# A diffusion layer's attention kernel: scratch transfers by pairs of heads

## The chip, the cores and the metric

The kernel runs on one core of one Trainium2 chip. The metric is device time in microseconds of one execution. The kernel before took 641.58 us (median of three runs, 641.37 to 641.83).

## What is computed

One layer over 1024 latent tokens (a grid of 16 rows by 64 columns) and 256 context tokens, model width 1024, in float32. The inputs are normalised and modulated, one projection gives eight groups of 512 columns, and two branches follow: attention in eight heads of 64, and a gated convolution. Cut to what matters here:

```python
h  = rmsnorm(x, norm_g) * (1 + scale) + shift          # (1024, 1024)
q, k, v, za, u, bg, cg, zc = split(h @ w_in)           # eight times (1024, 512)
q, k = rmsnorm(heads(q), q_norm_g), rmsnorm(heads(k), k_norm_g)
kc, vc = split(hc @ w_in[:, 512:1536])                 # context keys and values (256, 512)
# per head: scores of rotated q and k in an 8 x 16 window plus a bias,
# scores of plain q and kc, one softmax over both
s = concat([rope(q) @ rope(k_window) / 8 + bias, q @ kc / 8])
o = softmax(s) @ concat([v_window, vc])
attn = o * silu(za)
conv = bg * conv3(cg * u) * silu(zc)
out  = x + gate * (concat([attn, conv]) @ w_out)
```

## The kernel before

Matrix products keep float32 accuracy by splitting each operand into a high half and the rest (`halves`), and adding two or three products of those halves. A tensor in SBUF therefore often has a dimension of 2 for high and low.

There are four stages.

1. *Preparation.* Modulation, normalisation, transposing of the tokens, and the first convolution group.
2. *Projection of q, k and v.* The loop `for n in range(NT + 3)` runs over 4 pairs of heads times 8 tiles of 128 tokens. `proj_tile` gives a tile's products, `head_scale`, `rms_normed` and `rotated` finish q and k, `turn_qk` transposes them for every second tile, and `normed_ctx` and `turn_kc` do the context's keys and values once a pair. SBUF is full, so the results are spilled to scratch tensors in DRAM: `q_d`, `k_d`, `v_d`, `kc_d`, `vc_d`, one of each for a head. `spill` only notes a store; `flush`, at the next step of the loop, issues it on SP's queue.
3. *Attention.* The loop `for n in range(4 * NH + 4)` runs over quarters of heads, four to a head. `quarter(n)` writes out by hand, for all engines, the order of the work: the scores of quarter n, the exponentials of quarter n-2, the products with v of quarter n-3, and between them steps of `fill`, which are the products of the gate and convolution groups (tile `pu`, weights `uraw`). With `strict` on, TensorE, ScalarE, VectorE and GpSimd keep the written order. A class `head` loads its data from scratch: `load_v` at the head's first quarter, and for the following head `masks` and `load_q` (which also loads kc) in quarter 1 and `load_k` in quarter 2, as written. SP is not held to that order and issues a load when its turn has come and its buffer is free. Buffers for q, k, kc, v and the bias table are double: a head's buffers are those of the head two before it. q, k and kc are loaded twice over, once into partitions 0 to 63 and once into 64 to 127 (for q, the high half below and the low half above), so each of these is a transfer of 64 partitions. v's tile `vts` has 65 columns a block, the last of which holds a 1 in the high part and a 0 in the low part, so that the sum of the exponentials falls out as a 65th row of the product. That column is set once, and the loads fill the other 64 columns in rows of 256 bytes.
   `finish` copies a finished bank and stores it from ScalarE's queue (L1042, L1043). `gated` takes a pair's sums, inverts them, stores them to `ri_d`, and reads them back spread over 64 partitions a head by `load_sums`; the last pair does that on GpSimd's queue, in the fourth stage.
4. *Output projection.* `put_y` and `out_mm`, over two halves of the columns and eight tiles of tokens.

Line 55 is the helper through which ordered instructions are recorded, so many groups carry L55. The lines of the loads are L948 (k), L957 (q), L958 (kc), L965 and L967 (v), L507 (sums) and L295 (uraw).

Of the kernel before, what the change touches and what calls it, by code (L numbers as in the profile page):

```python
# [10 lines left out]
F32 = mybir.dt.float32  # L11
# [8 lines left out]
P = 128  # L20
D = 1024
T = 1024
# [17 lines left out]
def body(tc, es, x, ctxt, w_ada, b_ada, w_in, q_g, k_g, rpbr, w_out, vecs, cst, out):  # L40
# [49 lines left out]
    def many(name, n, shape):  # L90
        return [dr.tile(shape, F32, name=f"{name}{i}")[:] for i in range(n)]
# [9 lines left out]
    zs_d = many("zs_d", NPAIR, [P, T])  # L101


    q_d = many("q_d", NH, [2, HD, 4, 2, 256])
    k_d = many("k_d", NH, [HD, 4, 2, 256])
    v_d = many("v_d", NH, [P, 4, 2, 2 * HD])
    kc_d = many("kc_d", NH, [HD, 2, L])
    vc_d = many("vc_d", NH, [P, 2, 2 * HD])
    ri_d = many("ri_d", NPAIR, [2, T])


# [76 lines left out]
    def halves(dst, lo, src):  # L188
        act.copy(dst, src)
        dve.tensor_tensor(lo, src, dst.bitcast(F32), ALU.subtract)  # L190

    def put_v(vs, i, ps):

        halves(vs[:, :, 0, i], vs[:, :, 1, i], ps.rearrange("p (s d) -> p s d", s=2))

    def normed(qn, ps, scale, n):
        for h in range(n):
# [28 lines left out]
    def turn_qk(pp, p, two, t0):  # L226

        pA = psm.tile([P, 2, 2, P], F32, name="trA", tag="C", bufs=2)
        pB = psm.tile([P, 512], F32, name="trB", tag="C", bufs=2)
        for i, (qn, rot) in enumerate(two):  # L230
            pe.transpose(pA[:, 0, i], rot[:, 0:P], ident)
            pe.transpose(pA[:, 1, i], qn[:, 0:P], ident)
            pe.transpose(pB[:, i * P:(i + 1) * P], rot[:, P:256], ident)

        def put():
            qs = pp.tile([P, 2, 2, 256], F32R, name="qs", tag="qs", bufs=2)
            halves(qs[:, 0], qs[:, 1], pA[:].rearrange("p k i d -> p k (i d)"))
            ks = pp.tile([P, 2, 256], F32R, name="ks", tag="ks", bufs=2)
            halves(ks[:, 0], ks[:, 1], pB[:, :256])
            for s in range(2):  # L240
                h, rows = 2 * p + s, slice(64 * s, 64 * s + 64)
                for l in range(2):
                    spill(q_d[h][l, :, t0 // 2], qs[rows, l])
                spill(k_d[h][:, t0 // 2], ks[rows])
        return put

    def ctx_products(ch):
# [8 lines left out]
        return acc  # L256

    def normed_ctx(pp, acc, scales):
        two = []
        vs = pp.tile([P, 2, 2, 2, HD], F32R, name="vs", tag="vs", bufs=4)  # L260
        for i in range(2):
            qn = pp.tile([P, P], F32, name="kn", tag="kn", bufs=2)
            normed(qn, acc[i], scales[i], 2)
            pool.tensor_tensor(by_head(qn[:]), by_head(qn[:]), gkc.broadcast_to([P, 2, HD]), ALU.mult)
            put_v(vs, i, acc[i][:, P:256])
            two.append(qn)
        return two, vs

    def turn_kc(pp, p, two, vs):
        pB = psm.tile([P, 512], F32, name="trC", tag="C", bufs=2)  # L270
        for i in range(2):
            pe.transpose(pB[:, i * P:(i + 1) * P], two[i], ident)

        def put():
            ks = pp.tile([P, 2, 256], F32R, name="ks", tag="ks", bufs=2)
            halves(ks[:, 0], ks[:, 1], pB[:, :256])
            for s in range(2):
                h, rows = 2 * p + s, slice(64 * s, 64 * s + 64)
                spill(kc_d[h], ks[rows])
                spill(vc_d[h], vs[:, s].rearrange("p l i d -> p l (i d)"))  # L280
        return put

    def proj_tile(ch, t):
# [219 lines left out]
        pool.dma_start(ri_d[p].rearrange("h (x c) -> (h x) c", c=16), ri)  # L503

    def load_sums(f, half, rb, queue):
        for i in range(2):
            queue.dma_start(rb[64 * i:64 * i + 64],  # L507
                            ri_d[f][i:i + 1, half * 512:(half + 1) * 512].broadcast_to([64, 512]))


    prs = ExitStack()
# [421 lines left out]
                stores.append(lambda nh=nh, gr=gr: sp.dma_start(g_d[:, nh * 512:(nh + 1) * 512], gr[0:1]))  # L933


    class head:
        def __init__(self, h):
            self.h, self.p, self.s = h, h // 2, h % 2
# [5 lines left out]
        def load_k(self):  # L944
            h = self.h
            self.k = self.place().tile([P, 4, 2, 256], F32R, name="k_s", tag="A")
            for i in range(2):
                sp.dma_start(self.k[64 * i:64 * i + 64].bitcast(F32), k_d[h])  # L948

        def load_q(self):  # L950
            h = self.h
            self.q = self.place().tile([P, 2, T], F32R, name="q_s", tag="B")
            self.kc = bmp.tile([P, 2, L], F32R, name="kc_s", tag="kc_s", bufs=2)
            for i in range(2):
                rows = slice(64 * i, 64 * i + 64)
                for k in range(2):
                    sp.dma_start(self.q[rows, k].bitcast(F32).rearrange("p (t c) -> p t c", c=256), q_d[h][i, :, :, k])  # L957
                sp.dma_start(self.kc[rows].bitcast(F32), kc_d[h])  # L958

        def load_v(self):  # L960
            h = self.h
            self.v = vts[h % 2]
            for l in range(2):
                for t in range(4):
                    sp.dma_start(self.v[:, l, 2 * t:2 * t + 2, 0:HD].bitcast(F32),  # L965
                                 v_d[h][:, t, l].rearrange("p (b d) -> p b d", d=HD))
                sp.dma_start(self.v[:, l, NB:, 0:HD].bitcast(F32), vc_d[h][:, l].rearrange("p (b d) -> p b d", d=HD))  # L967

        def masks(self):
            self.bt = bmp.tile([P, 3, 384], F32, name="bt", tag="bt", bufs=2)  # L970
# [185 lines left out]
    pps = ExitStack()  # L1156
    pp = pps.enter_context(sbuf("ppn"))
    sq = pp.tile([P, 4, HD + 1], F32, name="sq")
    pool.memset(sq[:, :, HD:], EPS)
    rope = pp.tile([P, 2, NB, 2, HD], F32, name="rope")  # L1160
    sp.dma_start(rope[:].rearrange("p a b k d -> p (a b k d)"), rope_d)
# [8 lines left out]
    for n in range(NT + 3):  # L1170


        p, t = divmod(n, NB)
        at = 2 if p < NPAIR - 1 else 0
        if 1 <= t and p + 1 < NPAIR:
            raws += [chunk_load(CQ + (p + 1) * P, k) for k in ([t - 1] if t < NB - 1 else [t - 1, t])]
        if n == 0:
            loaded[z_col(4)] = unit_load(z_col(4))
        if n == NT - 8:
            loaded[z_col(0)] = unit_load(z_col(0))  # L1180
        if 1 <= n <= KT:
            gate.load(n - 1)
            next(spread, None)
        if 9 <= n < 25 and n % 2:
            next(tables)
        if n == NT - 6:
            heads[0].masks()
            heads[0].load_k()
        if n == NT - 5:
            heads[0].load_q()  # L1190
        flush()

        if t == 0 and 0 < n < NT:
            nxt += map(chunk_split, raws)
            ch, nxt, raws = nxt, [], []
        if n == 0:
            next(group0)
        if n == NT - 4:
            next(fill)
        if n < NT:  # L1200
            tiles[n] = proj_tile(ch, t)
        else:
            for _ in range((4, 3, 1)[n - NT]):
                next(fill)
        if 5 <= n < 9:
            for _ in range(2):
                next(group0)
        if n == 9:
            for _ in group0:
                pass  # L1210
        if 0 < n <= NT:
            scales[n - 1] = head_scale(pp, tiles[n - 1], 4)
            if n % 2:
                vs = pp.tile([P, 2, 2, 2, HD], F32R, name="vs", tag="vs", bufs=4)
            put_v(vs, (n - 1) % 2, tiles[n - 1][:, 256:384])
            if n % 2 == 0:
                q, r = divmod(n - 1, NB)
                for s in range(2):
                    spill(v_d[2 * q + s][:, r // 2], vs[:, s].rearrange("p l i d -> p l (i d)"))
        if t == at + 1 and n < NT:  # L1220
            cscales = [head_scale(pp, a, 2) for a in cacc]

        if 1 < n <= NT + 1:
            m, r = n - 2, (n - 2) % NB
            qn = rms_normed(pp, tiles[m], scales.pop(m))
        while waiting:
            waiting.pop(0)()
        if 4 <= t and p + 1 < NPAIR:
            nxt.append(chunk_split(raws.pop(0)))
        if 1 < n <= NT + 1:  # L1230
            tiles[m] = rotated(pp, rope, qn, r)
        if t == at + 2 and n < NT:
            kc = normed_ctx(pp, cacc, cscales)
        do_dves()
        if 2 <= n < KT + 2:
            gate.add(n - 2)
        if 9 <= n < 25 and n % 2 == 0:
            next(tables)
        do_acts()

        if n == KT + 5:
            gate.sum()
        if t == at and n < NT:
            cacc = ctx_products(ch)
        if n % 2 == 0 and n >= 4:
            waiting.append(turn_qk(pp, (n - 4) // NB, [tiles.pop(n - 4), tiles.pop(n - 3)], (n - 4) % NB))
        if t == at + 3 and n < NT:
            waiting.append(turn_kc(pp, p, *kc))
# [9 lines left out]
    prp = vs_.enter_context(sbuf("prp"))  # L1258
    vts = [prp.tile([P, 2, NB + 2, HD + 1], F32R, name=f"v{i}") for i in range(2)]
    fill_up(prp, 64)  # L1260
    for v in vts:
        for l in range(2):
            pool.memset(v[:, l, :, HD:HD + 1].bitcast(F32), 1.0 - l)

    gating = []

# [176 lines left out]
```

## Time and profile before

| | |
|---|---|
| median of three runs | 641.58 us (641.37 to 641.83) |
| the profiled execution's own time | 643.59 us |
| its span, first to last instruction | 641.8 us |
| instructions | 10295 |
| DMA packets | 118864, 125.46 MB, mean 195 GB/s |
| of these under 512 bytes, under 2 KB | 32817, 89353 |
| granted TensorE clock | 0.999 |

A profile shows one execution. Busy time counts the union of an engine's instructions; a wait is put down to what ended it; the chain is followed backwards from the last instruction through whatever released each step. A row of a view by stretches of time gives the length, the busy time of each engine, the granted clock, the mean busy share of the 16 DMA engines and GB/s.

### The profile page before, as it was taken

What the parts mean: (1) busy time and instruction counts of PE and PEld (TensorE: products, weight loads), DVE (VectorE), ACT (ScalarE), POOL (GpSimd) and SP (SyncE); (2) the same over time, 40 slices, a digit from 0 to 9 for tenths busy, and PEclk for the clock granted to TensorE, in tenths of its full rate; (3) what the DMA queues carried; (4) which work ended last, traced back from release to release, by engine and by line L of the source; (5) the groups of instructions that cost most, each with busy time, mean ns of one, the idle gap of its engine ahead of it and who ended that gap; (6) DMA issues with size and microseconds to landing.
All of it is one profiled execution on the core that took longest, in us unless ns stands there. A gap on an engine that the chain in (4) does not pass through costs nothing.

```text
span 641.8 us, 10295 instructions
## 1 busy us (share of the span) xinstructions
PE 629.1 (98%) x3480; PEld 537.3 (84%) x3480; DVE 432.3 (67%) x819; ACT 322.5 (50%) x692; POOL 131.5 (20%) x138
## 2 busy tenths in 40 slices
PE   8999999999999999999999999999999999999997
PEld 3477899999899999777688878888888888888885
DVE  1677859665756756458697889988998864565111
ACT  3676835424525444346676648565675644352000
POOL 1205024123123222001111211121111111004421
PEclk9999999999999999999999999999999999999999
DMA  8973647867785897899767758885862223965621
GB/s 319 379 257 97 180 121 259 256 188 206 241 260 165 271 269 218 216 221 223 184 160 195 186 140 212 202 214 149 225 150 88 71 81 128 293 235 198 215 100 49
DMA packets 118864, 125.46 MB, mean 195 GB/s; under 512 B 32817, under 2 KB 89353, under 8 KB 117532
## 3 DMA queue, kind: packets, MB, share of 16 engines
q1 hardware_dynamic: 112348, 113.23, 61.4%
q10 hardware_dynamic: 6208, 11.05, 5.5%
q0 software_dynamic: 256, 0.54, 0.3%
q8 instruction: 27, 0.44, 0.3%
q14 instruction: 25, 0.20, 0.1%
HBM read 88.01 MB, written 38.53 MB: 197 GB/s over the span
## 4 chain that ended last, share of the span: by engine, by line
PE 75%; DMA 10%; DVE 8%; SPq 3%; ACT 2%; issue 1%; ACTq 0%; DVEq 0%
PE pacc L55 21%; PE pu L55 18%; PE acc L55 5%; PE pout L76 5%; PE pout L74 5%; PE pout L75 5%; PE po L55 4%; PE tr L55 4%; PE cacc L55 4%; DMA v<-v_d 4%; DMA k_s<-k_d 3%; DVE mx L55 2%; DVE sb L55 2%; PE pss L55 2%; PE pmx L55 2%; DMA slab<-in_w_ada 2%
## 5 line engine op out<-in xcount | busy, mean ns | idle before, releaser
L55 PE MATMUL pu<-h,uh 128*128 128x512 f32 x544 | 169.0, 392 | 0.0
L55 PE MATMUL pacc<-wh,h 128*128 128x384 f32 x512 | 135.1, 338 | 0.0
L55 PEld LDWEIGHTS pu<-h,uh 128*128 128x128 f32 x544 | 98.2, 188 | 17.0
L55 PE MATMUL pu<-h,ul 128*128 128x512 f32 x272 | 106.3, 391 | 0.0
L55 PEld LDWEIGHTS pacc<-wh,h 128*128 128x128 f32 x512 | 92.8, 188 | 0.1
L55 POOL TENSOR_TENSOR plc<-sc,phc 128x512 fp32r<-128x512 f32 x32 | 42.5, 1327 | 222.8 <-ACT sc L55 111.4
L55 PE MATMUL pacc<-wl,h 128*128 128x384 f32 x256 | 85.6, 335 | 0.0
L55 POOL TENSOR_TENSOR ss<-ss,few 128x4 f32<-128x4 f32 (+1 forms) x40 | 42.0, 1051 | 125.8 <-DVE ss L55 125.4
L55 PEld LDWEIGHTS pu<-h,ul 128*128 128x128 f32 x272 | 51.1, 188 | 11.3
L55 DVE TENSOR_TENSOR mx<-mx,sb 128x384 f32<-128x384 f32 (+1 forms) x64 | 55.5, 876 | 1.9
L75 PE MATMUL pout<-wol,yh 128*128 128x512 f32 x128 | 49.8, 389 | 0.0
L76 PE MATMUL pout<-woh,yl 128*128 128x512 f32 x128 | 49.6, 389 | 0.0
L74 PE MATMUL pout<-woh,yh 128*128 128x512 f32 x128 | 48.3, 389 | 0.0
L55 PEld LDWEIGHTS pacc<-wl,h 128*128 128x128 f32 x256 | 48.1, 188 | 0.1
L55 DVE TENSOR_REDUCE ss<-sq 128x4 f32<-128x260 f32 (+1 forms) x40 | 15.7, 393 | 41.9 <-ACT sq L55 41.9
L55 ACT COPY mg<-pmx 128x256 f32<-128x256 f32 x32 | 12.0, 374 | 61.7 <-PE pmx L55 44.5
L55 ACT ACTIVATE sq<-pacc 128x256 f32<-128x256 f32 x32 | 12.3, 385 | 57.1 <-PE pacc L55 56.6
L1375 DVE TENSOR_TENSOR ot<-pout,gate 128x512 f32<-128x512 f32 x16 | 10.8, 688 | 37.6 <-PE pout L76 35.5
L55 DVE TENSOR_TENSOR pll<-sb,phl 128x768 fp32r<-128x768 f32 (+2 forms) x33 | 29.3, 889 | 7.9 <-ACT sb L55 7.9
L55 DVE TENSOR_TENSOR sc<-sc,mg 128x512 f32<-128x512 f32 x32 | 21.8, 683 | 19.0 <-ACT mg L55 19.0
L1376 POOL TENSOR_TENSOR ot<-ot,xr 128x512 f32<-128x512 f32 x15 | 20.0, 1347 | 67.6 <-DVE ot L1375 66.5
L55 ACT ACTIVATE qn<-pacc,ss 128x64 f32<-128x64 f32 x128 | 30.1, 329 | 4.7 <-issue 2.5
(151 smaller groups left out, 1277.0 us busy)
## 6 DMA issues: line engine op xcount, KB each, us to landing
uraw<-in_w_in SPq DMA_DIRECT2D x34, 256.0 KB
q_d<-qs SPq DMA_DIRECT2D x64, 128.0 KB
k_s<-k_d SPq DMA_DIRECT2D x16, 512.0 KB
q_s<-q_d SPq DMA_DIRECT2D x32, 256.0 KB
wr<-in_w_in SPq DMA_DIRECT2D x40, 192.0 KB
slab<-in_w_ada SPq DMA_DIRECT2D x6, 1024.0 KB
t_d<-btw SPq DMA_DIRECT2D x8, 576.0 KB
bt<-t_d SPq DMA_DIRECT2D x8, 576.0 KB
```

What stands on the lines that cost most here:

```text
L55: i = emit(*a, **kw)
L74: i = pe.matmul(ps, ah, bh, start=first, stop=False)
L75: pe.matmul(ps, ah, bl, start=False, stop=False)
L76: pe.matmul(ps, al, bh, start=False, stop=last)
L1375: dve.tensor_tensor(ot, ps, gate[:, cols], ALU.mult)
L1376: (dve if (nh, t) == (1, NB - 1) else pool).tensor_tensor(ot, ot, xr, ALU.add)
```

## The change

The scratch tensors are kept by pairs of heads, with 128 partitions. The stores of q, k and kc go out as one transfer for two heads. v's scratch holds all ten blocks (eight of latent tokens, two of context) with the columns of ones and zeros among them; the tile that is stored has them, and three such tiles are kept and used in turn. A head then loads v in two transfers, each a whole row of 650 numbers a partition. k and kc are read twice over by one transfer, whose source starts with a step of 0 and a count of 2 (`twice`). q's high and low parts come in one transfer for each of its two kinds (rotated and plain), the outermost dimension of whose source is the part. The sums of a pair's two heads are read by one transfer. A head has 7 loads in place of 19: one each of k, kc and the bias table, two of q and two of v.

```diff
-    q_d = many("q_d", NH, [2, HD, 4, 2, 256])
-    k_d = many("k_d", NH, [HD, 4, 2, 256])
-    v_d = many("v_d", NH, [P, 4, 2, 2 * HD])
-    kc_d = many("kc_d", NH, [HD, 2, L])
-    vc_d = many("vc_d", NH, [P, 2, 2 * HD])
+    q_d = many("q_d", NPAIR, [2, P, 4, 2, 256])
+    k_d = many("k_d", NPAIR, [P, 4, 2, 256])
+    v_d = many("v_d", NPAIR, [P, 2, 2, NB + 2, HD + 1])
+    kc_d = many("kc_d", NPAIR, [P, 2, L])
...
+    vss = []
+    def next_vs():
+        vss.append(vss.pop(0))
+        return vss[-1]
+    def spill_v(p, b, vs):
+        spill(v_d[p][:, :, :, b:b + 2].rearrange("p s l b d -> p (s l) (b d)"), vs.rearrange("p s l i d -> p (s l) (i d)"))
...
-            for s in range(2):
-                h, rows = 2 * p + s, slice(64 * s, 64 * s + 64)
-                for l in range(2):
-                    spill(q_d[h][l, :, t0 // 2], qs[rows, l])
-                spill(k_d[h][:, t0 // 2], ks[rows])
+            for l in range(2):
+                spill(q_d[p][l, :, t0 // 2], qs[:, l])
+            spill(k_d[p][:, t0 // 2], ks)
...
-            for s in range(2):
-                h, rows = 2 * p + s, slice(64 * s, 64 * s + 64)
-                spill(kc_d[h], ks[rows])
-                spill(vc_d[h], vs[:, s].rearrange("p l i d -> p l (i d)"))
+            spill(kc_d[p], ks)
+            spill_v(p, NB, vs)
...
     def load_sums(f, half, rb, queue):
-        for i in range(2):
-            queue.dma_start(rb[64 * i:64 * i + 64],
-                            ri_d[f][i:i + 1, half * 512:(half + 1) * 512].broadcast_to([64, 512]))
+        r = ri_d[f]
+        queue.dma_start(rb, bass.AP(r.tensor, r.offset + half * 512, [[T, 2], [0, HD], [1, 512]]))
...
+    def twice(rows):
+        n = 1
+        for step, size in list(rows.ap)[1:]:
+            n *= size
+        return bass.AP(rows.tensor, rows.offset, [[0, 2], [n, HD], [1, n]])
...
         def load_k(self):
-            for i in range(2):
-                sp.dma_start(self.k[64 * i:64 * i + 64].bitcast(F32), k_d[h])
+            sp.dma_start(self.k[:].bitcast(F32).rearrange("p t l c -> p (t l c)"), twice(k_d[self.p][64 * self.s:64 * self.s + 64]))
...
         def load_q(self):
-            for i in range(2):
-                rows = slice(64 * i, 64 * i + 64)
-                for k in range(2):
-                    sp.dma_start(self.q[rows, k].bitcast(F32).rearrange("p (t c) -> p t c", c=256), q_d[h][i, :, :, k])
-                sp.dma_start(self.kc[rows].bitcast(F32), kc_d[h])
+            for k in range(2):
+                sp.dma_start(self.q[:, k].bitcast(F32).rearrange("p (t c) -> p t c", c=256),
+                             q_d[self.p][:, 64 * self.s:64 * self.s + 64, :, k])
+            sp.dma_start(self.kc[:].bitcast(F32).rearrange("p l c -> p (l c)"), twice(kc_d[self.p][64 * self.s:64 * self.s + 64]))
...
         def load_v(self):
             for l in range(2):
-                for t in range(4):
-                    sp.dma_start(self.v[:, l, 2 * t:2 * t + 2, 0:HD].bitcast(F32),
-                                 v_d[h][:, t, l].rearrange("p (b d) -> p b d", d=HD))
-                sp.dma_start(self.v[:, l, NB:, 0:HD].bitcast(F32), vc_d[h][:, l].rearrange("p (b d) -> p b d", d=HD))
+                sp.dma_start(self.v[:, l].bitcast(F32), v_d[self.p][:, self.s, l])
...
+    vss += [pp.tile([P, 2, 2, 2, HD + 1], F32R, name=f"vs{i}")[:] for i in range(3)]
+    for v in vss:
+        for l in range(2):
+            pool.memset(v[:, :, l, :, HD:HD + 1].bitcast(F32), 1.0 - l)
...
-                vs = pp.tile([P, 2, 2, 2, HD], F32R, name="vs", tag="vs", bufs=4)
+                vs = next_vs()
...
-                for s in range(2):
-                    spill(v_d[2 * q + s][:, r // 2], vs[:, s].rearrange("p l i d -> p l (i d)"))
+                spill_v(q, r - 1, vs)
...
-    for v in vts:
-        for l in range(2):
-            pool.memset(v[:, l, :, HD:HD + 1].bitcast(F32), 1.0 - l)
```

More of the change, by code (lines that the diff above doesn't have):

```diff
@@ L190, in halves @@
         dve.tensor_tensor(lo, src, dst.bitcast(F32), ALU.subtract)
+    vss = []
[4 more added lines that the diff above has]
+        spill(v_d[p][:, :, :, b:b + 2].rearrange("p s l b d -> p (s l) (b d)"), vs.rearrange("p s l i d -> p (s l) (i d)"))
     def put_v(vs, i, ps):
-        halves(vs[:, :, 0, i], vs[:, :, 1, i], ps.rearrange("p (s d) -> p s d", s=2))
+        halves(vs[:, :, 0, i, :HD], vs[:, :, 1, i, :HD], ps.rearrange("p (s d) -> p s d", s=2))
     def normed(qn, ps, scale, n):
@@ L258, in normed_ctx @@
     def normed_ctx(pp, acc, scales):
-        two = []
-        vs = pp.tile([P, 2, 2, 2, HD], F32R, name="vs", tag="vs", bufs=4)
+        two, vs = [], next_vs()
         for i in range(2):
@@ L1213, in body @@
             if n % 2:
-                vs = pp.tile([P, 2, 2, 2, HD], F32R, name="vs", tag="vs", bufs=4)
+                vs = next_vs()
             put_v(vs, (n - 1) % 2, tiles[n - 1][:, 256:384])
```

## The prediction

> **What bounds the kernel now.** I read the page first, for the engines' shares and the chain.
>
> ```profile
> span 641.8 us, 10295 instructions
> PE 629.1 (98%) x3480; PEld 537.3 (84%) x3480; DVE 432.3 (67%) x819; ACT 322.5 (50%) x692; POOL 131.5 (20%) x138
> PE 75%; DMA 10%; DVE 8%; SPq 3%; ACT 2%; issue 1%; ACTq 0%; DVEq 0%
> ```
>
> TensorE is busy for 98% of the span and carries 75% of the chain that ended last; transfers carry only 10%. So making transfers cheaper can win little, and making them dear can lose much. Next, the stages: the attention stage cut at each head's first score product, by the busy time in stretches. The columns are length, then busy time of PE, PEld, DVE, ACT and POOL, the granted clock, the mean busy share of the 16 DMA engines, and GB/s.
>
> ```profile
> 270.23 0.48 PE L55 MATMUL pss<-q_s,k_s 128*128 128x256 f32 x2
> 481.88 0.72 PE L55 MATMUL pss<-q_s,k_s 128*128 128x256 f32 x4
> 223.80:270.20 46.40, 46.40 (x273) 44.20 (x272) 24.51 (x69) 20.20 (x75) 9.59 (x15) 1.00 0.88 235
> 270.20:481.90 211.70, 206.24 (x1177) 173.14 (x1175) 178.11 (x271) 136.64 (x223) 34.46 (x30) 1.00 0.77 190
> 481.90:641.80 159.90, 155.41 (x749) 129.27 (x747) 80.53 (x125) 51.84 (x86) 31.68 (x29) 1.00 0.44 146
> ```
>
> Head 0 starts at 270.2 and head 7 at 481.9, so seven heads take 211.7 us, 30.2 us each, or 7.6 us for each of a head's four quarters. In all of it TensorE stands idle for 211.70 - 206.24 = 5.5 us. That is the most that better loads can give back there. Then the chain in order of time, at the places where transfers stand on it, and the queue that issues them.
>
> ```profile
> 279.80 10.59 DMA k_s<-k_d
> 300.89 0.60 SPq L948
> 301.89 11.40 DMA v<-v_d
> 313.31 0.53 ACTq L1043
> 314.21 0.59 ACT sc L55
> 392.23 0.67 SPq L948 DMA_DIRECT2D k_s<-k_d  x1
> 396.08 0.46 SPq L948 DMA_DIRECT2D k_s<-k_d  x1
> 397.78 0.42 SPq L295 DMA_DIRECT2D uraw<-in_w_in  x1
> ```
>
> Two things are to be seen. ScalarE issues the stores of a finished bank (L1043), and it sat there until a v load that SP had queued behind a k load (L948) had landed; only then did its own arithmetic go on. And the weights of the filler products (uraw) are issued right behind the k load of the next head. Whatever holds that load holds those too, and ScalarE, which works in written order, must split them within the same head.
>
> **The change, part by part.** These are the transfers that it touches, with their counts and sizes.
>
> ```profile
> q_d<-qs SPq DMA_DIRECT2D x64, 128.0 KB
> k_s<-k_d SPq DMA_DIRECT2D x16, 512.0 KB
> q_s<-q_d SPq DMA_DIRECT2D x32, 256.0 KB
> v_d<-vs SPq DMA_DIRECT2D x32, 128.0 KB
> v<-v_d SPq DMA_DIRECT2D x64, 64.0 KB
> kc_s<-kc_d SPq DMA_DIRECT2D x16, 128.0 KB
> rb<-ri_d SPq DMA_DIRECT2D x12, 128.0 KB
> rb<-ri_d POOLq DMA_DIRECT2D x4, 128.0 KB, 3.7
> ```
>
> *Edits that I cost at nothing.* The stores of q, k and kc keep their bytes in half as many issues, the same rows. Each v store becomes 520-byte rows, four a partition, in place of 1 KB rows. All of it lies in the projection, where TensorE idles for none of the 46.40 us above; without that cover it would be some tenths of a microsecond a store. The three rotating v buffers in place of four, and six small memsets moved from the start of attention to the start of the projection, stand beside the same products; POOL is 20% busy. The v loads turn from ten of 256-byte rows into two of 2,600-byte rows, and gain at most a part of the 5.5 us. Each now needs its whole buffer free, which is so a quarter before the head starts, four quarters before its first use.
>
> *The loads of q, k, kc and 1/sum.* Here is the choice on which the forecast hangs. Before, each was cut into parts of 64 partitions, and 64 was the outermost count on both sides. Now one instruction fills 128 partitions, but its source pattern begins with a count of two: two copies for k and kc (`[[0, 2], [n, HD], [1, n]]`), the high and low plane for q, the two heads of 1/sum (`[[T, 2], ...]`). No transfer of before has that form at this size, so I bound it. One end: the 16 engines share it as they do now. Other end: the work is dealt out by the outermost count, and two engines carry everything. The nearest rows are four stretches in which the eight loads of the bias rows (248 rows each, whose largest divisor up to 16 is 8) run almost alone, and one in which transfers of 128 rows run.
>
> ```profile
> t_d<-in_rpb SPq DMA_DIRECT2D x8, 23.2 KB
> 72.00:73.00 1.00, 1.00 (x8) 0.84 (x7) 1.00 (x4) 0.49 (x2) 0.00 (x0) 1.00 0.25 28
> 73.00:74.00 1.00, 1.00 (x8) 0.63 (x7) 0.86 (x2) 1.00 (x2) 0.00 (x0) 1.00 0.38 47
> 74.00:75.00 1.00, 1.00 (x7) 0.82 (x6) 0.63 (x1) 1.00 (x3) 0.00 (x0) 1.00 0.30 37
> 75.00:76.00 1.00, 1.00 (x8) 0.87 (x7) 0.74 (x3) 1.00 (x3) 0.00 (x0) 1.00 0.27 33
> 10.00:14.00 4.00, 4.00 (x20) 1.39 (x17) 0.43 (x2) 2.27 (x4) 0.57 (x1) 1.00 1.02 412
> 276.00:292.00 16.00, 15.38 (x82) 12.76 (x81) 10.59 (x18) 10.52 (x17) 1.30 (x1) 1.00 1.00 215
> ```
>
> With 248 rows the share never passes 0.38; eight of 16 engines could give 0.5 at most. With 128 rows it is 1.02. That fits a deal by the outermost count; thin issue would explain it too. I take two engines: the only rows with an outermost count that 16 doesn't divide side with that reading. The Trainium skill says the same outright ("DMA: Bandwidth & Descriptors", section "Rules for kernel authors"): a leading zero-stride broadcast of c copies confines the whole transfer to at most c engines. The stretches above agree, and no run here shows it for two; by that rule the sum is the one below.
>
> *The price.* At full share an engine moves 412 / 16 = 25.7 GB/s (10:14, wide transfers) or 215 / 16 = 13.4 GB/s (276:292, where 64-partition loads crowd). Two engines alone crowd nobody, so I take 25.7. Per head, q is 4 x 256 KB and k 2 x 512 KB, 2,048 KB or 1,024 KB an engine, 1.05 MB: 41 us. kc adds 2 x 128 KB, 5 us: 46 us together, against 30.2 us for a whole head. 1/sum adds 4 x 128 KB a pair, or 5 us a head. These engines also owe their sixteenth of everything else: 190 GB/s over 30.2 us is 5.7 MB, less 2.4 MB of q, k and kc, leaves 3.3 MB, 0.21 MB an engine, 8 us.
>
> *Where it meets the path.* A head's q and k buffers come free when its successor's first scores are done, and only then are they refilled for the head after. So from one head's first scores to the next's lie at least the 46 us and, as an estimate, 3 us of issue, landing and score. The other three quarters do not all fit beside it. ScalarE stands at its bank store in quarter 1 until an older load lands, as at L1043 above, and the uraw behind k lands only after k, so the fillers and everything behind ScalarE stand too. I take two of the four quarters, 15 us, as work left when the loads are in. Period: 46 + 3 + 15 = 64 us, and the 8 us of other traffic runs in those 15. SP's queue stands behind the same landings; 12 fewer issues a head save nothing there.
>
> *Start and end.* Head 0's k load is issued at 223.8:
>
> ```profile
> 223.75 1.48 SPq L55 DMA_DIRECT2D k_s<-k_d  x2
> ```
>
> Its 46 us would just end at 270. But that stretch moves 235 GB/s x 46.4 us = 10.9 MB, of which 8.5 MB are others', 0.53 MB an engine, 20 us. So head 0 starts at 290. After head 7's first scores nothing large is left to load: 159.9 us stay. The last pair's 1/sum, on POOL's queue, goes from 3.7 us a load to 256 KB over two engines, 5 us, twice; it is needed by the seventh of eight rounds of the output products, which hide it.
>
> *Sum.* 290 + 7 x 64 + 160 = 898 us of span, 256 more than 641.8. The profiled execution took 643.6 us, 1.8 over its span and 2.0 over the median of 641.6. So I add 256 to the median: **898 us**.
>
> **The rivals.**
>
> *Well dealt (faster).* The 16 engines share the new transfers. Then 128 partitions an instruction replace pairs of 64, the crowded 13.4 GB/s an engine moves towards 25.7, k lands some 5 us earlier, and up to the 5.5 us of idle goes: 636 to 641 us. For it: the chain's 10.59 and 11.40 us pieces. It decides wherever a leading count of two doesn't limit the engines. The Trainium skill has a rule on this side too (same page and section): two transfers to disjoint partition halves had better be one of 128 partitions. The 13.4 against 25.7 GB/s agrees with it. Chance 0.08, of which 0.02 leave no measurable change (within 0.2%, about what a measurement here can tell).
>
> *Two engines, well hidden.* The transfers alone set the period, everything else fits beside them: 48 us, and head 0 is not late. 270 + 336 + 160 = 766 us. Against it stands ScalarE's wait at L1043. Chance 0.17 for times below 830.
>
> *Two engines, nothing hidden.* Other traffic and 1/sum stand in line as well: 46 + 3 + 13 + 15 = 77, with two and a half quarters left 81: 290 + 567 + 160 = 1017 us. Chance 0.15 for times above 950.
>
> *Two engines at the crowded rate.* 13.4 GB/s: 88 + 3 + 15 = 106 us a head, 290 + 742 + 160 = 1192 us. Against: only two engines write. Chance 0.05.
>
> **How the numbers follow.** The likeliest, 830 to 950 around 898, has 0.55. The range 766 to 1017 takes in the two neighbours and leaves out the well dealt case, the crowded rate and a little beside. Faster 0.06, same 0.02, slower 0.92.
>
> **What would show it.** Right: the k and q loads take some 20 us or more each to land; the DMA share of the attention stage falls from 0.77 to below 0.5 while the stage takes twice as long; TensorE's busy share drops to about 70%, its waits ending in k, q, uraw; the projection and the last 160 us look as before. Wrong: a share that stays at 0.7 or more with k landing in under 10 us means that all engines carry it, and the time is then near 638. A stage that grows by less than 100 us means that more lies beside the loads than I allowed.

## The result, and the profile after

The changed kernel took 918.93 us (median of four runs, 918.33 to 920.23) against 641.71 us before on the same chip: a ratio of 1.432, 95% interval 1.4295 to 1.4345. The forecast was 898 us, with a range of 766 to 1017.

The page of the changed kernel answers to the first lines shown of before (span, busy times, the chain by engine, and issues that were changed, with KB each and, where the trace has it, the median time to landing):

```profile
span 916.6 us, 10016 instructions
PE 655.5 (72%) x3479; PEld 558.7 (61%) x3480; DVE 429.1 (47%) x819; ACT 322.8 (35%) x692; POOL 129.4 (14%) x138
PE 49%; DMA 28%; SPq 12%; DVE 8%; ACT 2%; issue 2%; ACTq 0%; DVEq 0%
k_s<-k_d SPq DMA_DIRECT2D x8, 1024.0 KB
q_s<-q_d SPq DMA_DIRECT2D x16, 512.0 KB
rb<-ri_d POOLq DMA_DIRECT2D x2, 256.0 KB, 14.8
```

Fewer instructions, nearly the same bytes, and 275 us more. TensorE fell from 98% to 72%; on the chain, transfers rose from 10% to 28%, and SP's own issuing from 3% to 12%. The same three stages as before, cut at the first score products of head 0 and of head 7 (columns as in the prediction):

```profile
305.11 0.48 PE L55 MATMUL pss<-q_s,k_s 128*128 128x256 f32 x2
752.38 0.72 PE L55 MATMUL pss<-q_s,k_s 128*128 128x256 f32 x4
222.60:305.10 82.50, 51.76 (x278) 48.59 (x277) 24.23 (x69) 20.35 (x75) 9.72 (x11) 0.79 0.34 120
305.10:752.40 447.30, 227.07 (x1177) 191.23 (x1175) 174.98 (x271) 136.84 (x223) 34.04 (x30) 0.75 0.27 91
752.40:916.60 164.20, 157.02 (x749) 129.01 (x747) 80.72 (x125) 51.77 (x86) 31.27 (x27) 1.00 0.43 142
```

Where the time came from: head 0 starts 34.9 us later (305.1 for 270.2), the seven heads take 235.6 us more (447.3 for 211.7), and the end 4.3 us more (164.2 for 159.9). Together that is 274.8 us, the whole difference of the spans. In the seven heads the 16 engines are busy for 27% of the time, down from 77%, while the arithmetic waits for transfers. That pair, a low share and long waits for data, points to a few full engines and many empty ones. The packet records of the trace agree: for 60% of these 447.3 us exactly two packets are under way; before, it was 1% of the stage.

The waits of ScalarE and VectorE in that stretch (total, times, longest) show which data it was:

```profile
ACT uh L55 <- DMA uraw<-in_w_in: 74.0, 3, 34.8
ACT ub L55 <- DMA zs_d<-zs: 30.1, 1, 30.1
ACT mg L55 <- DMA q_s<-q_d: 22.7, 2, 15.7
DVE zs L55 <- DMA zs<-zs_d: 55.1, 2, 43.9
DVE zs L55 <- DMA rb<-ri_d: 38.4, 2, 32.0
DVE tb L55 <- DMA tb<-o_d: 25.8, 1, 25.8
```

Most of it is waited for weights (uraw) and gate rows (zs, tb), which the change doesn't touch. They stand behind the loads that it does touch, as the experiments below bear out. The 22.7 us ahead of mg are ScalarE standing at its bank store (L1046 in this kernel) until q had landed. And the chain from 218 to 306 us, where head 0's data are fetched, has SP itself as its longest pieces:

```profile
233.07 21.62 SPq L55
254.74 10.76 SPq L55
265.54 2.67 SPq L964
276.26 7.71 DMA k_d<-ks
```

SP was not waiting before an issue there, it stood 21.62 us inside the issue of q's second load and 10.76 us inside that of kc. Meanwhile the projection's stores were not issued, its buffers stayed full (ScalarE waited 31.2 us for a store of v), and TensorE ran for only 51.76 of 82.5 us. Head 0's first score product, at 305.11 above, waited for no data; it came when the late projection was through. In the seven heads the issues in SP's timeline add up to 274 of 447.3 us (106 issues); before, to 101 of 211.7 us (195 issues).

### The profile page after: what moved, and what is told of

Its sections match the earlier page's. It is cut to its first block, busy times and chain, and to the rows that moved or that the text cites. A ratio compares the mean times of both kernels' runs of the same rounds, so it can differ in the third digit from the quotient of the medians.

```text
span 916.6 us, 10016 instructions
## 1 busy us (share of the span) xinstructions
PE 655.5 (72%) x3479; PEld 558.7 (61%) x3480; DVE 429.1 (47%) x819; ACT 322.8 (35%) x692; POOL 129.4 (14%) x138
## 4 chain that ended last, share of the span: by engine, by line
PE 49%; DMA 28%; SPq 12%; DVE 8%; ACT 2%; issue 2%; ACTq 0%; DVEq 0%
PE pacc L55 12%; PE pu L55 12%; SPq L55 6%; DMA q_s<-q_d 5%; DMA zs_d<-zs 4%; DMA ri_d<-ri 4%; PE acc L55 4%; DMA zs<-zs_d 3%; PE po L55 3%; DMA tb<-o_d 3%; PE tr L55 3%; PE cacc L55 3%; DVE mx L55 2%; PE pout L76 2%; PE pout L75 2%; PE pout L74 2%
## 5 line engine op out<-in xcount | busy, mean ns | idle before, releaser
L55 PE MATMUL pu<-h,uh 128*128 128x512 f32 x544 | 171.7, 397 | 22.5 <-ACT ub L55 22.5
L55 PE MATMUL pmx<-ci,mx 128*128 128x128 f32 x64 | 17.1, 322 | 178.1 <-DVE mx L55 177.7
L55 PE MATMUL pacc<-wh,h 128*128 128x384 f32 x512 | 137.6, 343 | 0.0
L55 PEld LDWEIGHTS pmx<-ci,mx 128*128 128x128 f32 x64 | 9.6, 151 | 188.2 <-ACT sb L55 122.6
L55 DVE TENSOR_TENSOR ul<-uraw,uh 128x512 fp32r<-128x512 f32 x34 | 22.7, 683 | 97.2 <-ACT uh L55 97.0
L55 ACT ACTIVATE phc<-sc 128x512 fp32r<-128x512 f32 x32 | 20.2, 633 | 124.4 <-DVE sc L55 124.2
L55 DVE TENSOR_TENSOR mx<-mx,sb 128x384 f32<-128x384 f32 (+1 forms) x64 | 52.2, 824 | 2.0
L55 ACT CAST uh<-uraw 128x512 fp32r<-128x512 f32 x34 | 20.7, 615 | 83.3 <-DMA uraw<-in_w_in 83.2
L55 DVE TENSOR_TENSOR zs<-zs,rb 128x512 f32<-128x512 f32 x6 | 4.1, 689 | 93.5 <-DMA zs<-zs_d 55.1
L55 PE MATMUL pss<-q_s,k_s 128*128 128x384 f32 (+1 forms) x128 | 34.4, 398 | 16.8 <-DMA k_s<-k_d 16.8
```

The costliest lines, as they stand in the source:

```text
L55: i = emit(*a, **kw)
```

## The experiments

Each edit is shown against the changed kernel, unless said otherwise. Times are medians; the ratio is to the kernel before on the same chip, with its 95% interval.

**All loads in halves again.** Pair scratch, 128-partition stores and v's whole rows stay.

```diff
-            sp.dma_start(self.k[:]..., twice(k_d[self.p][64 * self.s:64 * self.s + 64]))
+            for i in range(2):
+                sp.dma_start(self.k[64 * i:64 * i + 64]..., k_d[self.p][64 * self.s:64 * self.s + 64])
...                                                # the same for q (by part), kc and 1/sum
```

> The loads of q, k, kc and 1/sum are cut into two transfers of 64 partitions again, so that no source begins with a count of two; the scratch by pairs, the stores of 128 partitions, v's columns of ones, the three v buffers and the whole-row v loads stay as in the changed kernel. Theory (the leading count of two puts these loads on two of 16 engines): the time falls from 919 us back to 634 to 643 us, the share of the DMA engines in the attention stage is back above 0.6. Rival (something else in the change costs it: the shared scratch of two heads, three v buffers, v loads that need the whole buffer): still above 850 us. A mixture would lie between and tell how much each has.

640.43 us, ratio 0.9973 (0.9959 to 0.9988). Head 0 and head 7 start at 270.4 and 478.7:

```profile
270.40:478.70 208.30, 204.64 (x1176) 173.27 (x1175) 178.12 (x271) 136.68 (x223) 34.81 (x30) 1.00 0.69 188
478.70:638.70 160.00, 155.46 (x750) 129.38 (x748) 80.44 (x125) 51.81 (x86) 31.64 (x29) 1.00 0.45 146
```

The whole loss lies in the form of these loads, and none in the rest. The rest gains 1 to 3 us: the heads take 208.3 us in place of 211.7, with 3.7 us of idle TensorE for 5.5. This version is 0.3% faster than the kernel before.

**The count by itself.** A kernel of loads alone:

```python
dims = [[4096, P], [1, 2048]] if c == P else [[0, c], [4096, P // c], [1, 2048]]
nc.sync.dma_start(big, bass.AP(w_in.tensor, w_in.offset, dims))      # then VectorE reads big
```

> Only loads, one at a time, each waited for by VectorE: the same 1 MB into 128 partitions by rows of 8 KB, from sources whose outermost count is 128, 64, 32, 16, 8, 4 and 2 (all but the first read rows more than once), then the same in two transfers of 64 partitions; all of that twice. The layer isn't computed. Theory (engines are dealt by the outermost count, up to 16): 128 to 16 take the same, 4 to 6 us; 8 takes 7, 4 takes 12, 2 takes 22 us, with DMA shares near 0.5, 0.25 and 0.12 in between; the two halves 5 to 7 us. Rival (all engines share any transfer of 128 partitions): all between 4 and 7 us.

The second round, in the timeline. The wait is the last number; the counts are 128, 64, 32, 16, 8, 4, 2, then the two halves:

```profile
88.74 0.15 DVE L49 COPY few<-big 128x1 f32<-128x1 f32 x1 [4.91 <-DMA big<-in_w_in]
94.09 0.15 DVE L49 COPY few<-big 128x1 f32<-128x1 f32 x1 [5.20 <-DMA big<-in_w_in]
99.51 0.15 DVE L49 COPY few<-big 128x1 f32<-128x1 f32 x1 [5.26 <-DMA big<-in_w_in]
106.99 0.15 DVE L49 COPY few<-big 128x1 f32<-128x1 f32 x1 [7.32 <-DMA big<-in_w_in]
119.18 0.15 DVE L49 COPY few<-big 128x1 f32<-128x1 f32 x1 [12.04 <-DMA big<-in_w_in]
136.61 0.15 DVE L49 COPY few<-big 128x1 f32<-128x1 f32 x1 [17.28 <-DMA big<-in_w_in]
159.12 0.15 DVE L49 COPY few<-big 128x1 f32<-128x1 f32 x1 [22.36 <-DMA big<-in_w_in]
166.79 0.15 DVE L49 COPY few<-big 128x1 f32<-128x1 f32 x1 [7.52 <-DMA big<-in_w_in]
```

In stretches of the first round (counts 128, 8, 4 and 2; here the columns are DVE, POOL, clock, DMA share, GB/s):

```profile
1.50:5.50 4.00, 0.00 (x0) 0.00 (x0) 1.00 0.75 262
25.00:34.50 9.50, 0.00 (x0) 0.00 (x0) 1.00 0.48 110
37.00:53.00 16.00, 0.00 (x0) 0.00 (x0) 1.00 0.22 63
56.00:75.50 19.50, 0.00 (x0) 0.00 (x0) 1.00 0.12 53
```

0.48, 0.22 and 0.12 lie near 8, 4 and 2 of 16 engines (0.50, 0.25, 0.125). With a count of two, 53 GB/s is 26.5 an engine, close to the rate that the prediction took (25.7). Counts of 16, 8 and 4 took longer than forecast (7.3, 12.0, 17.3 for 4 to 6, 7, 12 us); with 8 and 4 an engine moved only 13.8 and 15.8 GB/s (110 / 8, 63 / 4), and why stays open. Two halves of 64 take 7.5 us for 4.9: the crowding is real. The repeated reading of one row alone does not cost: 32 copies took 5.3 us.

**One kind of load at a time.** The edit of the first experiment, but k and kc, or q, or 1/sum, keep the count of two.

> As the changed kernel, but q and 1/sum in halves of 64 partitions; k and kc alone keep the leading count of two. Theory: two engines owe k and kc 1,280 KB / 2 = 0.66 MB or 26 us a head at 25.7 GB/s, and some 10 us of other traffic; the period of a head goes from 30 us to between 30 (all hidden) and 26 + 3 + 15 = 44 us, so 645 to 745 us, I take 690. Rival (the loads of 20 us and more hold up SP's queue by their number and not by their bytes): as bad as half of the whole loss, about 780 us.

> As the changed kernel, but k, kc and 1/sum in halves; q alone keeps the leading count of two. Theory: 1,024 KB / 2 = 0.52 MB or 21 us a head on two engines and 10 us of other traffic, about one period of 30 us: 640 to 710 us, I take 665. If the losses added up by bytes, q, k with kc and 1/sum would share the 277 us as 41 : 51 : 10 hundredths; if the period is a maximum of two things, each alone costs much less than its share. Rival as for the kernel with k: about 780 us.

> As the changed kernel, but q, k and kc in halves of 64 partitions; 1/sum alone keeps the leading count of two. Theory: 512 KB a pair on two engines, 10 us twice five microseconds apart, for three pairs; the last pair on POOL's queue has its loads hidden by the output products. 640 to 660 us, I take 647. If it costs over 20 us, the 1/sum loads stand on the path in full, and so does the last pair's.

k and kc alone: 744.49 us, ratio 1.1586 (1.1541 to 1.163), at the upper end of what was expected. q alone: 781.30 us, 1.2159 (1.2127 to 1.2191), 116 us over the guess and outside its range. 1/sum alone: 647.96 us, 1.0075 (1.005 to 1.0099). Over the version with halves that is 104, 141 and 8 us, 253 of the whole 278. So the parts nearly add up. The rivals' 780 us fits q and is 36 us too high for k. The idea that a load of 21 us would hide beside 30 us of work was wrong. Why, the chain of the kernel with q shows, and its longest waits for data:

```profile
373.93 26.11 DMA q_s<-q_d
400.06 0.45 ACTq L1049
417.46 7.82 SPq L964
425.33 21.71 DMA k_s<-k_d
447.06 0.45 ACTq L1049
ACT mg L55 <- DMA k_s<-k_d: 40.0, 2, 21.7
ACT mg L55 <- DMA q_s<-q_d: 29.1, 2, 14.8
```

The k load here goes in halves over all engines, yet takes 21.71 us. SP stands 7.82 us in an issue of q (L964) and then 11.38 us in k's two issues; the rest is argued to be k's share on the two engines, behind q's rows. Each landing is followed by ScalarE's bank store (L1049 here), which stood until then: four times, 69.1 us in all. That is the wait that the prediction had at L1043; why a store on ScalarE's queue waits for these loads, no run shows.

**q from another queue, and q behind k.** From the kernel with q alone:

```diff
-                sp.dma_start(self.q[:, k]...               # first: POOL's queue
+                pool.dma_start(self.q[:, k]...
...
-                for load in ((nx.masks, nx.load_q), (nx.load_k,), ())[g - 1]:    # second: k ahead of q
+                for load in ((nx.masks, nx.load_k), (nx.load_q,), ())[g - 1]:
```

> As the kernel in which q alone keeps the count of two (781 us), but q's loads are issued from POOL's queue. Theory (q's 21 us a head would fit beside 30 us of work; what costs 139 us is that every transfer behind q on SP's queue gets its sixteenth behind q's rows on the two engines, and that SP stands in the issue of the next one until there is room): with a queue of its own q delays the others little, 645 to 690 us. Rival (two engines' bytes themselves set the time, whatever the queue): 760 to 790 us again. POOL's own arithmetic may be late by the writing of the descriptors, some microseconds a head.

> As the kernel in which q alone keeps the count of two (781 us), with the loads of k written ahead of those of q and kc, one quarter earlier. Bytes, engines and queue are the same. Theory (the cost is what stands behind q's rows on the first two engines): k no longer stands behind q, but uraw, zs, kc and the rest still do; 700 to 760 us, if SP's queue takes the new order. Rival (q itself is late and sets the period): 775 to 790 us, as before.

POOL's queue: 670.30 us, 1.0432 (1.0401 to 1.0463), so 111 of the 141 us go. k ahead of q: 755.79 us, 1.1771 (1.1731 to 1.181), 26 us less with the same bytes on the same queue. Both agree with the queue and not with the bytes. The first is not clean: POOL's queue may use other engines than SP's. So the next kernel was to ask about the queue alone.

**What lands behind.** Loads only: q's two loads of 512 KB, then a small one of 256 KB.

```python
load(queue, 0); load(queue, 1)     # halves on SP; count of two on SP, on POOL, on ScalarE
nc.sync.dma_start(z, x[0, 0:P, 0:512])
```

> Only loads: a small transfer (128 partitions, 256 KB) on SP's queue, alone and behind q's two loads in five forms, each group waited for by VectorE, all of it twice; the layer isn't computed. Groups: the small one alone; behind q in four halves of 64 partitions on SP; behind q with the count of two on SP; beside the same on POOL's queue; beside the same on ScalarE's queue. Theory (a queue is served in order on each engine, so a transfer has landed only when its share behind q's rows on the first two engines has): 2 to 4 us alone, 6 to 10 us behind the halves, 24 to 28 us behind the count of two on SP, with SP standing several microseconds in an issue; 3 to 10 us beside POOL's or ScalarE's queue, since the engines serve the queues in turn. Rival (what is held is SP itself, by the issue, and nothing on the engines): the small one lands 3 us after its own issue in each group, however late that issue is.

The timeline (zz is the small one, qq are q's; SPq, POOL and ACTq lines are issues), first the group with the count of two on SP, then its counterparts on POOL's and on ScalarE's queue:

```profile
9.65 7.27 SPq L54 DMA_DIRECT2D qq<-in_w_in  x2
16.97 10.63 SPq L63 DMA_DIRECT2D zz<-in_x  x1
22.35 0.15 DVE L50 COPY few<-qq 128x1 f32<-128x1 f32 x1 [12.38 <-DMA qq<-in_w_in]
33.42 0.15 DVE L50 COPY few<-qq 128x1 f32<-128x1 f32 x1 [10.93 <-DMA qq<-in_w_in]
33.97 5.21 POOL L54 DMA_DIRECT2D qq<-in_w_in  x2 [33.52 <-DVE qq L76]
34.04 0.15 DVE L50 COPY few<-zz 128x1 f32<-128x1 f32 x1 [0.40 <-DMA zz<-in_x]
34.29 0.33 SPq L63 DMA_DIRECT2D zz<-in_x  x1
36.84 0.15 DVE L50 COPY few<-zz 128x1 f32<-128x1 f32 x1 [2.58 <-DMA zz<-in_x]
48.94 0.15 DVE L50 COPY few<-qq 128x1 f32<-128x1 f32 x1 [11.95 <-DMA qq<-in_w_in]
52.90 0.15 DVE L50 COPY few<-qq 128x1 f32<-128x1 f32 x1 [3.80 <-DMA qq<-in_w_in]
53.14 0.33 SPq L63 DMA_DIRECT2D zz<-in_x  x1
53.20 8.32 ACTq L54 DMA_DIRECT2D qq<-in_w_in  x2
55.75 0.15 DVE L50 COPY few<-zz 128x1 f32<-128x1 f32 x1 [2.58 <-DMA zz<-in_x]
```

On SP's own queue the small transfer landed at 34.0, right behind q's last row and 24.4 us after the group began. Alone it took 2.7 us, behind the four halves 8.5 us. SP stood 7.27 us inside q's two issues and 10.63 us inside the small one's own, together 17.9 of the 24.4 us; 6.4 us more passed after that issue, where 2.3 pass when it is alone. So most of the delay is the rival's, SP held by its issues, and some 4 us are the theory's, a share behind q's rows on the engines. The count of two brings both: SP was through with q's four halves, the same bytes, in 2.60 us.

The groups on POOL's and ScalarE's queue don't answer their question. There SP issued the small transfer 0.3 us after POOL's first issue began, and just before ScalarE's (53.14 and 53.20). It was through, or nearly, when q's first rows moved (37.4 and 55.0 us by the packet records), and its 2.6 us are those of a transfer alone. Whether another queue lets a transfer past rows that already stand on the engines is not shown here. POOL's two loads landed 3.8 us apart in place of 10.9: 1.05 MB within 18.9 us of the first issue is more than the 53 GB/s of two engines, so they had more than two, and part of the 111 us belongs to that.

The Trainium skill ("DMA: Bandwidth & Descriptors", section "Issuing engines are not separate DMA queues") says that issuing from several engines only saves the sequencer's time, which is usually small beside the transfer. Here it was not small: from head 0's to head 7's start the issues in SP's timeline add up to 185 of 337.6 us with q on SP's queue, and to 58 of 239.1 us with q on POOL's. How much of the 111 us is that, and how much the other engines, was not separated.

**Better forms of the loads.** Scratch in 128 even rows, so that one load of 128 partitions needs no count of two: for q alone, and for q, k and kc (the last two stored twice). Then the gate's loads moved to POOL's queue, on the version with halves and on the one with q.

```diff
-    q_d = many("q_d", NPAIR, [2, P, 4, 2, 256])
+    q_d = many("q_d", NH, [2, HD, 4, 2, 256])
...
+                sp.dma_start(self.q[:, k]..., q_d[h].rearrange("i d t k c -> (i d) t k c")[:, :, k])
...
-            sp.dma_start(zs, zs_d[f][:, cols])             # the last two kernels, also tb and 1/sum
+            pool.dma_start(zs, zs_d[f][:, cols])
```

> As the one before, but only q has scratch with 128 rows in one even step; k, kc and 1/sum are loaded in halves from scratch by pairs. No stores are added. Theory: 637 to 641 us, a little better than all in halves (640.4), because q's loads land sooner and SP issues two fewer a head. Rival: the same as all in halves, since nothing waits for q there.

> What the change wanted without a count of two: scratch of q, k and kc by heads with 128 rows in one even step (k and kc stored twice, q's two parts one behind the other), so that one load of 128 partitions has 128 as its outermost count; stores in parts of 64 partitions; v as in the changed kernel; 1/sum in halves. Theory: all 16 engines at the uncrowded rate, k and q land in about 3 us less than as halves, and of the 5.5 us of idle time some comes back: 636 to 640 us. Rival (the doubled stores of k fill SP's queue and the engines in the projection, whose products wait then): 642 to 650 us.

> As the kernel with all loads in halves (640.4 us), with the gate's loads in the attention stage (zs, o and 1/sum of the first three pairs) issued from POOL's queue, so that they do not stand behind k on SP's. Theory: the waits of VectorE for zs and of ScalarE behind them shrink, 637 to 640 us. Rival (POOL's arithmetic waits behind those issues, or the two queues share the same engines and nothing is gained): 640 to 646 us.

> As the kernel with q's scratch in 128 even rows (647 us), with the same loads issued from POOL's queue. That kernel lost 5 us in the head in which zs of the second pair was issued right behind k and took 10 us to land. Theory: that loss goes, 637 to 641 us. Rival (the order on SP's queue only moves the wait elsewhere): 645 to 648 us.

All four missed: 646.98 us (ratio 1.007, 1.0052 to 1.0088), 651.37 (1.0155, 1.0124 to 1.0186), 642.87 (1.0011, 0.9997 to 1.0025) and 651.89 (1.0149, 1.0115 to 1.0183). In the first, one head takes 38 us for 33 with halves, and its chain and SP's queue show where:

```profile
386.63 1.26 SPq L958 DMA_DIRECT2D k_s<-k_d  x2
388.57 1.39 SPq L1285 DMA_DIRECT2D zs<-zs_d  x1
388.57 10.02 DMA zs<-zs_d
```

With fewer issues ahead of it, SP sent k earlier, and the gate's zs came to stand behind it. A sooner landing of q bought nothing, since nothing waited for q. That moving zs away would cure it was argued, and the fourth kernel didn't bear it out: there zs, on POOL's queue and issued 0.4 us after k, still took 9.75 us to land. So its place on SP's queue alone did not make zs late. The second kernel loses most in head 0, 34.5 us for 26.2: uraw is issued at 284.5, behind the doubled stores, and ScalarE waits 11.1 us for it, much as the rival had it.

## Why the prediction was right

*The choice of two engines* held: the shares of 0.12, 0.22 and 0.48 and the return to 640.4 us with halves show it. So did *the rate* (25.7 GB/s taken, 26.5 measured).

*The period of a head*, 64 us forecast, was 447.3 / 7 = 63.9 us. That is nearer than its terms deserve, and partly luck: single heads took 46.3 to 78.1 us. The term of the transfers is about right: in the loads-only kernels q's pair took 23.8 us (9.65 to 33.42) and 1 MB with a count of two, as k is, 22.4 us, together 46 for the 41 taken. The 15 us of unhidden quarters were put on ScalarE's bank store (L1043) and on uraw. Both were there, with 22.7 and 74.0 us over the seven heads, or 13.8 a head. But the gate's rows, zs, 1/sum and tb, were waited for longer (119 us of VectorE's waits), and SP stood inside its issues; the prediction had neither in this sum. Such waits lie partly beside the transfers and beside each other, so the trace doesn't give 64 as a sum of these terms.

*Head 0's start* was the step that failed: 290 forecast, 305.1 measured. It charged two engines with 20 us of other traffic, let head 0 wait for its loads, and left TensorE's projection running beside them. SP stood 32 us in two issues there, the stores stood too, the projection itself came late (51.76 us busy of 82.5), and the first score product waited for it and not for the loads. Those 15 us and 4 at the end are the 19 us between 898 and the 916.6 of the span. At the end 1/sum took 14.8 us to land on POOL's queue for 5 a load forecast, but no engine waited for it; the longest transfer on the chain there is tb from y_d, 12.41 us at 819.18, and what cost the 4 us was not separated.

*The edits costed at nothing* agree with the version in halves, 640.4 us. The price of the "well dealt" rival (636 to 641 us) is not borne out: with loads of 128 partitions for q alone, and for q, k and kc, dealt to all engines, it was 647 and 651 us.

*What would show it*: TensorE at 72% for 70, the share at 0.27 for "below 0.5", the stage 2.1 times as long for twice. The waits for data ended less in q and k (39.5 us in the seven heads) than in uraw and the gate's rows. "The projection looks as before" was wrong.

## What to carry to other kernels

Before joining transfers, look at the outermost count of both sides: here one instruction in place of two went from 16 engines to two because its source began with a 2. A falling DMA share together with growing waits for data is how the trace shows it, and the waits name whatever is queued behind, not the culprit. All the rest of the change, fewer issues among it, was worth about 2 us here, the form of these loads 278.

## What the runs showed of the hardware that was not expected

- An issue can hold its queue. SP stood up to 21.62 us inside one load whose two engines still had rows to move, and nothing else left that queue meanwhile.
- A transfer over all engines lands late behind a narrow one on its queue: 21.71 us for a k load in halves behind q, 24.4 us for a load of 256 KB that takes 2.7 alone. For 11.4 and 17.9 us of these SP was inside issues.
- While TensorE waited, its granted clock fell. In a stretch of 25 us without products it was 0.50:

```profile
567.00:592.00 25.00, 0.00 (x0) 0.00 (x0) 0.00 (x0) 0.00 (x0) 0.00 (x0) 0.50 0.27 99
```

The same 1177 products of the seven heads took 227.07 us of busy time in place of 206.24; how much of those 20.8 us is the clock and how much is lost overlap was not separated.
